# Outer-product mixer's attention on 32-key tiles: five levels and the diagonal in four column positions, the larger distances in one step

## Chip, core and metric

The kernel runs on one core of a Trainium2 chip. The metric is the device time of one execution in microseconds (us); lower is better. Before the change the median of three runs is 1098.15 us (1097.73 to 1098.18).

## What is computed

A trunk of two layers over 256 positions and 2048 channels: RMS norms, an input projection, token mixers, gates, an output projection, gated embeddings. The change touches one mixer of the first layer, `hgrn2`: eight heads with 128 key and 128 value channels. Cut to its core, for one head and a chunk of positions:

```python
f = lb + (1.0 - lb) * sigmoid(fp)          # decay per position and channel
k = (1.0 - lb) * sigmoid(-fp)
b = cumsum(log(f))
w[t, s, d] = exp(b[t, d] - b[s, d])         # s <= t, else 0
attn[t, s] = sum_d q[t, d] * k[s, d] * w[t, s, d]
o[t] = (q * exp(b))[t] @ state + attn[t] @ v
```

So the score of query t and key s carries, channel by channel, the product of the decays f at positions s+1 to t. The reference walks in chunks of 64 with a state; the kernel computes the whole lower triangle of the 256 positions instead.

## The kernel before

All large projections run on TensorE in two pieces of the operands. A weight tile `raw` arrives by DMA, ScalarE casts its high part `whi` (L123), VectorE subtracts to get the remainder `wlo` (L124). `block` (a 128-column block of output, features on partitions) runs sixteen matmuls of 512 columns with `whi` (L154), then calls `pump()`, then sixteen of 256 columns with `wlo` (L160). There are four `whi`, four `wlo` and five `raw` buffers, and a block uses two of each, so the casts run up to two blocks ahead. `merge` (L166, L167) adds the two halves. `project` is two blocks. `project_tok` (tokens on partitions, L195 to L197) pumps once for each quarter of the weights.

`pump()` is what sets the order of the work around the change. Smaller pieces of work are written as generators in lanes ("att" the attention, "rg" the linear recurrence `rg_lru`, "pl" the embeddings' norm, and others). Each pump advances every lane by one `yield`; what it issues stands on TensorE between L154 and L160 of that block. The order on each engine is then fixed by a scheduler when the program is built.

The attention runs for two groups of four heads. `attention(0)` is started before the projections of f and q for group 1 (eight blocks), and so lies between them; `attention(1)` is started after them and lies in the eight blocks of `xb_proj` and the `project_tok` of the gate (`gate_tok`), beside `rg_lru`. For one group f, q and k are 128 channels by 1024 columns, that is four heads of 256 positions, or eight chunks c of 128. The scores are built by levels: at level B the keys of the even blocks of B positions meet the queries of the odd blocks beside them, after both were scaled to the border between them by products of decays (`tot`). The steps of one group, a pump each:

- an empty one, then the diagonal: eight matmuls of 128 keys by 128 queries (L544) into two PSUM tiles `mx`, multiplied by the identity into the score tile `A` (L545), and q times f (L547);
- levels 1, 2, 4, 8 and 16: for each chunk one matmul with all 128 keys as weights and the 64 odd queries streaming (L560), then q and k are multiplied by `tot` (L567, L568), the next `tot` is made (L571), and a masked copy puts the wanted scores into `A` (L578);
- levels 32 and 64: two matmuls of 32 keys or one of 64 keys a chunk (L557), which write PSUM partitions 0 and 64, or 0; plain copies into `A` (L575);
- the cross half: keys of the first 128 positions with queries of the second (L585), copied by ScalarE to `Ac` (L587);
- `read_out`: scores times values (L608, L611), sums of squares and norm.

A float32 matmul of the program is two matmul instructions in the trace, each with a load of weights. PSUM tiles `mx` come from a pool of three, which `rg_lru` (L646, then ScalarE's sigmoids, L650) uses too.

Of the kernel before, what the change touches and what calls it, by code (L numbers as in the profile page):

```python
# [11 lines left out]
F32 = mybir.dt.float32  # L12
F32R = mybir.dt.float32r
I32 = mybir.dt.int32
U32 = mybir.dt.uint32
AF = mybir.ActivationFunctionType
ALU = mybir.AluOpType
PSUM = bass.MemoryType.PSUM

P = 128  # L20
T = 256
# [15 lines left out]
    PRM[_n] = (_o, _w)  # L37
    _o += _w
NPRM = _o
LEVELS = [1, 2, 4, 8, 16, 32, 64]  # L40
MASKED = [b for b in LEVELS if b < 32]
NCST = 128 + 64 * len(MASKED) + 256 + 64


@with_exitstack
def trunk(ctx: ExitStack, tc: tile.TileContext, a, out):
    nc = tc.nc
    v, s, gp, te, sy = nc.vector, nc.scalar, nc.gpsimd, nc.tensor, nc.sync
# [7 lines left out]
    px = ctx.enter_context(tc.tile_pool(name="px", bufs=3, space=PSUM))  # L56
# [36 lines left out]
    gp.memset(eps, EPS)  # L93
    ident = cst[:, 0:128]
    c0 = 128
    lmask = {}
    for b in MASKED:
        lmask[b] = cst[:, c0:c0 + 64].bitcast(U32)
        c0 += 64
    tri2 = cst[:, c0:c0 + 256]  # L100
    c0 += 256
    sel8 = cst[:, c0:c0 + 64].rearrange("p (h m) -> p h m", m=8)

    def pc(name, i=0, n=None):
        o, w = PRM[name]
# [289 lines left out]
    m0 = m0_scope.enter_context(tc.tile_pool(name="m0", bufs=2))  # L395
# [55 lines left out]
    def gate_tok(w, j, act, u):  # L451
# [6 lines left out]
    mx, e0, e1, lb, omb, sp, ez, z2, pol, sp8, spm8 = (small(8, n) for n in (  # L458
        "mx", "e0", "e1", "lb", "omb", "sp", "ez", "z2", "pol", "sp8", "spm8"))
# [38 lines left out]
    with m0_scope:  # L498
        ew = a["ew"]
        fs, qs, ks = [], [], []  # L500
        for g in range(2):
            f = m0.tile([P, 1024], F32, name="f", tag="f")
            k = m0.tile([P, 1024], F32, name="k", tag="k")
            q = m0.tile([P, 1024], F32, name="q", tag="q")
# [26 lines left out]

        res = {}

        def attention(g):

            f, q, k = fs[g], qs[g], ks[g]
            A = m0.tile([P, 8, P], F32, name="A", tag="A", bufs=1)
            Ac = m0.tile([P, 4, P], F32, name="Ac", tag="Ac", bufs=1)
            yield
            for b in range(2):  # L540
                ps = px.tile([P, 512], F32, name="mx", tag="mx")
                for c in range(4):
                    o = (b * 4 + c) * P
                    te.matmul(ps[:, c * P:(c + 1) * P], k[:, o:o + P], q[:, o:o + P], start=True, stop=True)  # L544
                v.tensor_tensor(out=A[:, b * 4:b * 4 + 4, :], in0=ps.rearrange("p (c t) -> p c t", c=4),  # L545
                                in1=ident.unsqueeze(1).to_broadcast([P, 4, P]), op=ALU.mult)
            v.tensor_tensor(out=q, in0=q, in1=f, op=ALU.mult)  # L547
            yield
            tot = f
            for B in LEVELS:  # L550
                ps = px.tile([P, 512], F32, name="mx", tag="mx")
                for c in range(8):
                    o = c * P
                    if B >= 32:

                        for x in range(0, P, 2 * B):
                            te.matmul(ps[x:x + B, c * 64:c * 64 + B], k[:, o + x:o + x + B],  # L557
                                      q[:, o + x + B:o + x + 2 * B], start=True, stop=True)
                    else:
                        te.matmul(ps[:, c * 64:(c + 1) * 64], k[:, o:o + P],  # L560
                                  q[:, o:o + P].rearrange("p (n two b) -> p n two b", two=2, b=B)[:, :, 1, :],
                                  start=True, stop=True)
                n = 512 // B
                tv = tot.rearrange("p (n two) -> p n two", two=2)
                qv = q.rearrange("p (n two b) -> p n two b", two=2, b=B)[:, :, 1, :]
                kv = k.rearrange("p (n two b) -> p n two b", two=2, b=B)[:, :, 0, :]
                v.tensor_tensor(out=qv, in0=qv, in1=tv[:, :, 0:1].to_broadcast([P, n, B]), op=ALU.mult)  # L567
                v.tensor_tensor(out=kv, in0=kv, in1=tv[:, :, 1:2].to_broadcast([P, n, B]), op=ALU.mult)  # L568
                if B < 64:
                    nt = m0.tile([P, n], F32, name=f"tot{B}", tag=f"tot{B}", bufs=1)  # L570
                    v.tensor_tensor(out=nt, in0=tv[:, :, 0], in1=tv[:, :, 1], op=ALU.mult)  # L571
                    tot = nt
                if B >= 32:
                    for x in range(0, P, 2 * B):
                        v.tensor_copy(A[x:x + B, :, x + B:x + 2 * B],  # L575
                                      ps.rearrange("p (c b) -> p c b", c=8)[x:x + B, :, 0:B])
                else:
                    v.copy_predicated(  # L578
                        A.rearrange("p c (n two b) -> p c n two b", two=2, b=B)[:, :, :, 1, :],
                        lmask[B].rearrange("p (n b) -> p n b", b=B).unsqueeze(1).to_broadcast([P, 8, 64 // B, B]),  # L580
                        ps.rearrange("p (c n b) -> p c n b", c=8, b=B))
                yield
            ps = px.tile([P, 512], F32, name="mx", tag="mx")
            for c in range(4):
                te.matmul(ps[:, c * P:(c + 1) * P], k[:, c * T:c * T + P], q[:, c * T + P:(c + 1) * T],  # L585
                          start=True, stop=True)
            s.copy(Ac.rearrange("p c t -> p (c t)"), ps)  # L587
            yield
            read_out(g, A, Ac, vts[g])

# [8 lines left out]

        def read_out(g, A, Ac, vt):  # L600

# [115 lines left out]
    for i in range(4):  # L717
        t = hp.tile([P, 1024], F32, name="hq", tag="h")
# [12 lines left out]
    with tc.tile_pool(name="m1", bufs=2) as m1:  # L731
# [34 lines left out]
        ps = pm.tile([P, 512], F32, name="mm", tag="mm")  # L766
        for hf in range(2):
# [124 lines left out]
        for j in range(4):  # L892
            ps = project_tok(a["oog"], j, acth)
# [132 lines left out]
        banks = []  # L1026
# [9 lines left out]
        for hf, ps in enumerate(quarter(1, [(hf, kq) for hf in range(2) for kq in range(4)])):  # L1036
            pl = pls[3][hf][:, T:2 * T]
            gated(4, ps[hf], banks[hf][:, T:2 * T], pl, hf, hf == 0)
            x = hss[:, 4, hf:hf + 1]
            p0 = pre[:, hf:hf + 1]  # L1040
            y, yh, t, r = (tp.tile([P, 1], F32, name=n, tag=n, bufs=2) for n in ("fy", "fyh", "ft", "fr"))
# [10 lines left out]
            for g in (3, 1, 0, 2):  # L1052
                o = pls[g][hf]
# [27 lines left out]
def _const():  # L1081
    c = np.zeros((P, NCST), np.float32)
    c[:, 0:128] = np.eye(P, dtype=np.float32)
    o = 128
    si = np.arange(P)[:, None]
    j = np.arange(64)[None, :]
    for b in MASKED:
        c[:, o:o + 64] = (si // (2 * b) == j // b) & ((si // b) % 2 == 0)
        o += 64
    c[:, o:o + P] = np.where(si <= np.arange(P)[None, :], 0.0, -1e30)  # L1090
    o += 256
    for h in range(8):
        c[:, o + h * 8 + h] = 1.0
    return c


# [70 lines left out]
```

## Time and profile before

| | |
|---|---|
| median of three runs | 1098.15 us |
| span of the profiled execution, first to last instruction | 1096.9 us |
| TensorE (PE) busy | 1075.8 us, 98% |
| VectorE (DVE) busy | 763.6 us, 70% |
| ScalarE (ACT) busy | 570.9 us, 52% |
| GpSimd (POOL) busy | 84.1 us, 8% |
| attention group 0 | 121 to 188 us |
| attention group 1 | 194 to 267 us |

The profiled execution's own time beside its span is not listed apart; its span is 1.25 us under the median of the runs. PE rows are matmuls, PEld rows loads of weights, which overlap with them. Matmul ends are modelled and matmuls overlap, so the distance between starts tells more than the length of one.

### The profile page before, as it was taken

The page shows a single profiled execution, that of the slowest core. Times are in us where ns is not written, and L with a number is a line of the kernel's source. Part 1 is how long each engine was busy: PE and PEld are TensorE (multiplying, and loading weights), DVE is VectorE, ACT ScalarE, POOL GpSimd, SP SyncE. Part 2 cuts the span into 40 slices and gives each one's busy share as a digit, 9 for nine tenths or more (in the row PEclk, how much of TensorE's full clock was granted, in tenths as well). Part 3 has the DMA queues.
Part 4 walks back from the last instruction along what each step waited for, and adds up shares of the span by engine and source line. Part 5 has one row for each costly group of instructions (what it writes and reads, how often), then busy time and mean ns, then how long its engine had stood idle before and what let it go on. Part 6 is the DMA issues. An engine that isn't in the chain of part 4 may idle for free.

```text
span 1096.9 us, 15476 instructions
## 1 busy us (share of the span) xinstructions
PE 1075.8 (98%) x5850; PEld 927.7 (85%) x5850; DVE 763.6 (70%) x1119; ACT 570.9 (52%) x828; POOL 84.1 (8%) x69
## 2 busy tenths in 40 slices
PE   7999999999999999999999999999999999999996
PEld 7788898988888888888888888888888877888886
DVE  7868977887877656777544877765457687655665
ACT  6565435567655435555444666554444554434443
POOL 2143200000100000112000000000000121000111
PEclk9999999999999999999999999999999999999998
DMA  8655534444765555565654654455555755555652
GB/s 322 217 180 192 183 130 151 151 135 141 240 204 186 190 192 191 189 195 172 196 196 153 197 166 154 151 167 193 192 192 191 224 201 172 192 183 182 190 175 77
DMA packets 55947, 200.37 MB, mean 183 GB/s; under 512 B 6208, under 2 KB 6464, under 8 KB 55872
## 3 DMA queue, kind: packets, MB, share of 16 engines
q1 hardware_dynamic: 54720, 195.18, 53.6%
q0 software_dynamic: 1152, 4.19, 1.2%
q8 instruction: 46, 0.75, 0.3%
q14 instruction: 29, 0.24, 0.1%
HBM read 197.25 MB, written 2.10 MB: 182 GB/s over the span
## 4 chain that ended last, share of the span: by engine, by line
PE 93%; DVE 5%; ACT 1%; issue 1%; DMA 0%; SPq 0%; DVEq 0%; ACTq 0%
PE mm L154 32%; PE mm L160 17%; PE mm L195 12%; PE mm L197 12%; PE mm L196 12%; DVE wlo L124 2%; PE mx L560 2%; PE mm L1020 1%; PE mm L1018 1%; PE mm L1019 1%; PE nu L859 1%; ACT whi L123 1%; PE mx L646 1%; DVE ahl L139 0%; DMA raw<-in_pw_dram 0%
## 5 line engine op out<-in xcount | busy, mean ns | idle before, releaser
L124 DVE TENSOR_TENSOR wlo<-raw,whi 128x1024 fp32r<-128x1024 f32 (+1 forms) x361 | 451.0, 1273 | 232.0 <-ACT whi L123 133.8
L123 ACT CAST whi<-raw 128x1024 fp32r<-128x1024 f32 (+1 forms) x361 | 376.6, 1047 | 334.9 <-PE mm L154 174.0
L154 PE MATMUL mm<-ahl,whi 128*128 128x512 f32 x1536 | 367.6, 391 | 2.7 <-DVE ahl L448 1.9
L154 PEld LDWEIGHTS mm<-ahl,whi 128*128 128x128 f32 x1536 | 282.1, 188 | 59.3 <-DVE ahl L448 3.0
L195 PE MATMUL mm<-whi,ahl 128*128 128x512 f32 x608 | 239.5, 394 | 0.8 <-DVE u L456 0.7
L197 PE MATMUL mm<-whi,ahl 128*128 128x512 f32 x608 | 236.9, 390 | 0.9 <-DVE ahl L139 0.9
L196 PE MATMUL mm<-wlo,ahl 128*128 128x512 f32 x608 | 237.1, 390 | 0.0
L160 PE MATMUL mm<-ahl,wlo 128*128 128x256 f32 x1536 | 202.3, 285 | 0.0
L160 PEld LDWEIGHTS mm<-ahl,wlo 128*128 128x128 f32 x1536 | 195.2, 191 | 6.1
L197 PEld LDWEIGHTS mm<-whi,ahl 128*128 128x128 f32 x608 | 114.1, 188 | 25.7 <-DVE ahl L139 1.8
L195 PEld LDWEIGHTS mm<-whi,ahl 128*128 128x128 f32 x608 | 114.2, 188 | 25.4 <-DVE u L456 1.5
L196 PEld LDWEIGHTS mm<-wlo,ahl 128*128 128x128 f32 x608 | 114.2, 188 | 23.4 <-DVE wlo L124 0.7
L166 ACT COPY sm<-mm 128x256 f32<-128x256 f32 x64 | 23.7, 370 | 53.7 <-PE mm L160 53.7
L272 POOL TENSOR_TENSOR acc<-acc,sq 128x512 f32<-128x512 f32 x11 | 18.1, 1642 | 214.2 <-ACT sq L271 214.0
L167 DVE TENSOR_TENSOR mg<-mm,sm 128x256 f32<-128x256 f32 x64 | 26.5, 415 | 0.1
L744 DVE SCALAR_TENSOR_TENSOR qk<-mg,prm,qk 128x255 f32<-128x255 f32 (+2 forms) x48 | 21.2, 478 | 6.9 <-ACT qk L741 6.5
L911 POOL DMA_DIRECT2D row<-in_rows_dram x4 | 2.2, 554 | 279.9 <-DVE u L943 268.1
L1006 POOL TENSOR_TENSOR pl<-pl,row 128x512 f32<-128x512 f32 x6 | 9.2, 1532 | 153.6 <-ACT sq L990 153.6
L447 ACT ACTIVATE ahl<-mx,prm 128x256 fp32r<-128x256 f32 x24 | 11.0, 473 | 18.0 <-DVE ahl L448 9.9
L560 PEld LDWEIGHTS mx<-q,k 128*128 128x128 f32 x160 | 19.4, 191 | 0.8
L560 PE MATMUL mx<-q,k 128*128 128x64 f32 x160 | 18.9, 271 | 0.0
L1018 PE MATMUL mm<-whi,ahl 128*128 128x256 f32 x64 | 18.3, 285 | 0.0
(281 smaller groups left out, 824.0 us busy)
## 6 DMA issues: line engine op xcount, KB each, us to landing
raw<-in_ew_dram SPq DMA_DIRECT2D x64, 512.0 KB, 4.5
raw<-in_g_dram SPq DMA_DIRECT2D x56, 512.0 KB, 3.9
raw<-in_eo_dram SPq DMA_DIRECT2D x32, 512.0 KB, 4.3
raw<-in_ov_dram SPq DMA_DIRECT2D x32, 512.0 KB, 3.8
raw<-in_oqk_dram SPq DMA_DIRECT2D x32, 512.0 KB, 4.2
raw<-in_oog_dram SPq DMA_DIRECT2D x32, 512.0 KB, 3.9
raw<-in_oz_dram SPq DMA_DIRECT2D x32, 512.0 KB, 3.9
raw<-in_oo_dram SPq DMA_DIRECT2D x32, 512.0 KB, 4.3
```

The lines of the kernel that those rows point to most:

```text
L123: last["act"] = s.copy(h, r).ins
L124: last["dve"] = v.tensor_tensor(out=l, in0=r, in1=h.bitcast(F32), op=ALU.subtract).ins
L154: last["pe"] = te.matmul(ps, parts[k // 8][0][:, c:c + P], act[k // 2][2][:, (k % 2) * 512:(k % 2 + 1) * 512], start=(k == 0), stop=False).ins
L160: last["pe"] = te.matmul(ps[:, T:2 * T], parts[k // 8][1][:, c:c + P], act[k // 2][0][:, k % 2], start=False, stop=(k == KT - 1)).ins
L166: s.copy(small, ps[:, T:2 * T])
L167: v.tensor_tensor(out=dst, in0=ps[:, 0:T], in1=small, op=ALU.add)
L195: te.matmul(ps[hf], xh, wh, start=(k == 0), stop=False)
L196: te.matmul(ps[hf], xh, wl, start=False, stop=False)
L197: last["pe"] = te.matmul(ps[hf], xl, wh, start=False, stop=(k == KT - 1)).ins
L560: te.matmul(ps[:, c * 64:(c + 1) * 64], k[:, o:o + P], q[:, o:o + P].rearrange("p (n two b) -> p n two b", two=2, b=B)[:, :, 1, :], start= ...
L744: v.scalar_tensor_tensor(dst[:, sh:T], pi[:, 0:T - sh], pc("ccw", k * 16 + b), dst[:, sh:T], op0=ALU.mult, op1=ALU.add)
L1018: te.matmul(ps[hf], xh, wh, start=(k == 0), stop=False)
```

## The change

The last two levels go, and the diagonal moves into the first level. Everything within 32 positions is now computed on tiles of 32 keys: a matmul has 32 keys as weights, streams 16 queries (32 for the diagonal), and writes one of four groups of 32 PSUM partitions (the column positions 0, 32, 64 and 96 of the array). Their results go to a small tile `C` of 32 columns a chunk, by masked copies of 128 columns in all, and ScalarE copies `C` into the diagonal blocks of `A`. The last step does all larger distances at once: pairs of neighbouring 32-blocks straight from k and qf, blocks two and three apart with copies scaled once more (`k64`, `q64`, which reuse the tile of `tot`), and the cross half with copies `kx`, `qx` (which reuse f), scaled by running products of the four decays of a half (`sx`, `pf`, first filled by GpSimd). q times f goes to a tile of its own, `qf`. `A` is made once, zeroed by GpSimd. A group now takes eight pumps instead of eleven.

```diff
-LEVELS = [1, 2, 4, 8, 16, 32, 64]
+LEVELS = [1, 2, 4, 8, 16]
...
+        A = m0.tile([P, 8, P], F32, name="A", tag="A", bufs=1)
+        gp.memset(A, 0.0)
...
-            for b in range(2):
-                ps = px.tile([P, 512], F32, name="mx", tag="mx")
-                for c in range(4):
-                    te.matmul(ps[:, c * P:(c + 1) * P], k[:, o:o + P], q[:, o:o + P], start=True, stop=True)
-                v.tensor_tensor(out=A[:, b * 4:b * 4 + 4, :], in0=ps.rearrange("p (c t) -> p c t", c=4),
-                                in1=ident.unsqueeze(1).to_broadcast([P, 4, P]), op=ALU.mult)
-            v.tensor_tensor(out=q, in0=q, in1=f, op=ALU.mult)
+            v.tensor_tensor(out=qf, in0=q, in1=f, op=ALU.mult)
             yield
...
+                if B == 1:
+                    for c in range(8):
+                        for x in range(0, P, 32):
+                            o = c * P + x
+                            te.matmul(ps[x:x + 32, 128 + c * 32:160 + c * 32], k[:, o:o + 32], q[:, o:o + 32],
+                                      start=True, stop=True)
                 for c in range(8):
-                    if B >= 32:
-                        for x in range(0, P, 2 * B):
-                            te.matmul(ps[x:x + B, c * 64:c * 64 + B], k[:, o + x:o + x + B],
-                                      q[:, o + x + B:o + x + 2 * B], start=True, stop=True)
-                    else:
-                        te.matmul(ps[:, c * 64:(c + 1) * 64], k[:, o:o + P],
-                                  q[:, o:o + P].rearrange("p (n two b) -> p n two b", two=2, b=B)[:, :, 1, :],
+                    for x in range(0, P, 32):
+                        o = c * P + x
+                        te.matmul(ps[x:x + 32, c * 16:(c + 1) * 16], k[:, o:o + 32],
+                                  qf[:, o:o + 32].rearrange("p (n two b) -> p n two b", two=2, b=B)[:, :, 1, :],
                                   start=True, stop=True)
...
+            for x in range(0, P, 32):
+                s.copy(A[x:x + 32, :, x:x + 32], C[x:x + 32])
+            yield
+            for b in range(2):
+                ps = px.tile([P, 512], F32, name="mx", tag="mx")
+                for i in range(4):
+                    c = 4 * b + i
+                    for x, kk, y_, qq in ((0, k4[:, c, 0], 1, q4[:, c, 1]), (1, k4[:, c, 1], 2, q4[:, c, 2]),
+                                          (2, k4[:, c, 2], 3, q4[:, c, 3]), (0, k64[:, c], 2, q4[:, c, 2]),
+                                          (1, k4[:, c, 1], 3, q64[:, c]), (0, k64[:, c], 3, q64[:, c])):
+                        te.matmul(p3[32 * x:32 * x + 32, i, 32 * y_:32 * y_ + 32], kk, qq, start=True, stop=True)
...
+                te.matmul(ps[:, cc], kx[:, cc], qx[:, cc], start=True, stop=True)
+            for b, p3 in enumerate(banks):
+                for x in range(3):
+                    r = slice(32 * x, 32 * x + 32)
+                    s.copy(A[r, 4 * b:4 * b + 4, 32 * x + 32:P], p3[r, :, 32 * x + 32:P])
             s.copy(Ac.rearrange("p c t -> p (c t)"), ps)
             yield
             read_out(g, A, Ac, vts[g])
```

TensorE at the end of group 0, from level 16 on, before (a row is line, operation, output and inputs, shape of the output, count of matmuls of the program; `mm` rows are the projection's):

```order
L560 MATMUL mx<-q,k 128x64 x8
L160 MATMUL mm<-ahl,wlo 128x256 x16
L154 MATMUL mm<-ahl,whi 128x512 x16
L557 MATMUL mx<-q,k 32x32 x16
L160 MATMUL mm<-ahl,wlo 128x256 x16
L154 MATMUL mm<-ahl,whi 128x512 x16
L557 MATMUL mx<-q,k 64x64 x8
L160 MATMUL mm<-ahl,wlo 128x256 x16
L154 MATMUL mm<-ahl,whi 128x512 x16
L585 MATMUL mx<-q,k 128x128 x4
```

The same place now, with the first of the last step's eight chunks (`tot_1344` is the tile of `k64` and `q64`; line numbers are those of the changed kernel, where the projection's L154 and L160 are L153 and L159):

```order
L556 MATMUL mx<-qf,k 32x16 x32
L159 MATMUL mm<-ahl,wlo 128x256 x16
L153 MATMUL mm<-ahl,whi 128x512 x16
L615 MATMUL mx<-qf,k 32x32 x3
L615 MATMUL mx<-qf,tot_1344 32x32
L615 MATMUL mx<-tot_1344,k 32x32
L615 MATMUL mx<-tot_1344 32x32
```

Two pumps with a block each have gone from between level 16 and the cross half. The blocks themselves are as many as before, so they now stand elsewhere: what follows in the lane comes earlier.

ScalarE in group 1 around the cross half, before (`it` and `av` are `rg_lru`'s sigmoids, `u` the gate's, `tt` its tanh, `whi` the casts of weights):

```order
L650 ACTIVATE it<-mx,prm 128x256 x2
L123 CAST whi<-raw 128x1024
L455 ACTIVATE u<-mm,rth 128x512
L587 COPY Ac<-mx 128x512
L656 ACTIVATE tt<-av,sp_257 128x256 x2
L657 ACT_TABLE_LOAD
L657 ACTIVATE av<-av,spm_258 128x256
L123 CAST whi<-raw 128x1024 x2
```

And now, from the second bank's copies to the next cast of weights:

```order
L624 COPY A<-mx 32x4x96
L624 COPY A<-mx 32x4x64
L624 COPY A<-mx 32x4x32
L625 COPY Ac<-mx 128x512
L694 ACTIVATE tt<-av,sp_257 128x256
L688 ACT_TABLE_LOAD
L688 ACTIVATE av<-mx,prm 128x256 x2
L688 ACTIVATE it<-mx,prm 128x256 x2
L165 COPY sm<-mm 128x256
L695 ACT_TABLE_LOAD
L695 ACTIVATE av<-av,spm_258 128x256
L122 CAST whi<-raw 128x1024
```

The cross half of group 1 moved from the gate's first tiles back between the blocks of `xb_proj`, into the middle of `rg_lru`'s activations, and three copies for each bank stand ahead of `Ac`.

More of the change, by code (lines that the diff above doesn't have):

```diff
@@ L95, in trunk @@
     c0 = 128
+    ident32 = cst[:, c0:c0 + 32]
+    c0 += 32
     lmask = {}
-    for b in MASKED:
-        lmask[b] = cst[:, c0:c0 + 64].bitcast(U32)
-        c0 += 64
+    for b in LEVELS:
+        lmask[b] = cst[:, c0:c0 + 16].bitcast(U32)
+        c0 += 16
     tri2 = cst[:, c0:c0 + 256]
-    c0 += 256
-    sel8 = cst[:, c0:c0 + 64].rearrange("p (h m) -> p h m", m=8)
     def pc(name, i=0, n=None):
@@ L568, in attention @@
                 v.tensor_tensor(out=kv, in0=kv, in1=tv[:, :, 1:2].to_broadcast([P, n, B]), op=ALU.mult)
[L569 to L581, printed above, removed]
@@ L582, in attention @@
-                yield
+                nt = m0.tile([P, n], F32, name=f"tot{B}", tag=f"tot{B}", bufs=1)
+                v.tensor_tensor(out=nt, in0=tv[:, :, 0], in1=tv[:, :, 1], op=ALU.mult)
+                if B == 1:
+                    v.tensor_tensor(out=C, in0=ps[:, 128:384].rearrange("p (c t) -> p c t", c=8),
+                                    in1=ident32.unsqueeze(1).to_broadcast([P, 8, 32]), op=ALU.mult)
+                    t1 = nt
+                tot = nt
+                v.copy_predicated(
+                    C.rearrange("p c (n two b) -> p c n two b", two=2, b=B)[:, :, :, 1, :],
+                    lmask[B].rearrange("p (n b) -> p n b", b=B).unsqueeze(1).to_broadcast([P, 8, 16 // B, B]),
+                    ps[:, 0:128].rearrange("p (c n b) -> p c n b", c=8, b=B))
@@ new lines, in attention @@
+                if B < 16:
+                    yield
+            tb = tot.rearrange("p (c b) -> p c b", b=4)
+            t4 = tot.rearrange("p (h two b) -> p h two b", two=2, b=4)
+            sx = m0.tile([P, 4, 4], F32, name="sx", tag="sx", bufs=1)
+            pf = m0.tile([P, 4, 4], F32, name="pf", tag="pf", bufs=1)
+            gp.memset(sx[:, :, 3:4], 1.0)
+            gp.memset(pf[:, :, 0:1], 1.0)
+            v.tensor_copy(sx[:, :, 2], t4[:, :, 0, 3])
+            v.tensor_copy(pf[:, :, 1], t4[:, :, 1, 0])
@@ new lines, in attention @@
+            for i in (1, 0):
+                v.tensor_tensor(out=sx[:, :, i], in0=sx[:, :, i + 1], in1=t4[:, :, 0, i + 1], op=ALU.mult)
+                j = 3 - i
+                v.tensor_tensor(out=pf[:, :, j], in0=pf[:, :, j - 1], in1=t4[:, :, 1, j - 1], op=ALU.mult)
+            k64, q64 = (t1[:, i * T:(i + 1) * T].rearrange("p (c s) -> p c s", s=32) for i in range(2))
+            kx, qx = (f[:, i * 512:(i + 1) * 512] for i in range(2))
+            k4 = k.rearrange("p (c b s) -> p c b s", b=4, s=32)
@@ new lines, in attention @@
+            q4 = qf.rearrange("p (c b s) -> p c b s", b=4, s=32)
+            k5 = k.rearrange("p (h two b s) -> p h two b s", two=2, b=4, s=32)
+            q5 = qf.rearrange("p (h two b s) -> p h two b s", two=2, b=4, s=32)
+            v.tensor_tensor(out=k64, in0=k4[:, :, 0], in1=tb[:, :, 1:2].to_broadcast([P, 8, 32]), op=ALU.mult)
+            v.tensor_tensor(out=q64, in0=q4[:, :, 3], in1=tb[:, :, 2:3].to_broadcast([P, 8, 32]), op=ALU.mult)
+            v.tensor_tensor(out=kx.rearrange("p (h b s) -> p h b s", h=4, s=32), in0=k5[:, :, 0],
+                            in1=sx.unsqueeze(3).to_broadcast([P, 4, 4, 32]), op=ALU.mult)
@@ L1085, in _const @@
     si = np.arange(P)[:, None]
[L1086 to L1089, printed above, removed]
+    j = np.arange(16)[None, :]
+    c[:, o:o + 32] = si % 32 == np.arange(32)[None, :]
+    o += 32
+    for b in LEVELS:
+        c[:, o:o + 16] = (si % 32 // (2 * b) == j // b) & ((si // b) % 2 == 0)
+        o += 16
     c[:, o:o + P] = np.where(si <= np.arange(P)[None, :], 0.0, -1e30)
-    o += 256
-    for h in range(8):
-        c[:, o + h * 8 + h] = 1.0
     return c
```

20 lines of the change are left out of this document (11 added, 9 removed).

## Prediction

> **What bounds the kernel now.** I read the page first: its totals, the share of each engine, and the chain that ended last.
>
> ```profile
> span 1096.9 us, 15476 instructions
> PE 1075.8 (98%) x5850; PEld 927.7 (85%) x5850; DVE 763.6 (70%) x1119; ACT 570.9 (52%) x828; POOL 84.1 (8%) x69
> PE 93%; DVE 5%; ACT 1%; issue 1%; DMA 0%; SPq 0%; DVEq 0%; ACTq 0%
> ```
>
> TensorE is busy in 98% of the span and carries 93% of the chain, so work taken off it shortens the kernel wherever nothing else is late. Next I read the chain in order of time through the attention, where each step stands between the sixteen L154 and the sixteen L160 matmuls of a projection block (columns: start, length, what).
>
> ```profile
> 112.58 3.65 PE mm L154 x16
> 116.23 1.91 PE mm L160 x16
> 118.14 3.66 PE mm L154 x16
> 121.80 1.78 PE mx L544 x16
> ...
> 125.49 3.65 PE mm L154 x16
> 129.15 1.73 PE mx L560 x16
> ...
> 132.84 3.65 PE mm L154 x16
> ...
> 162.22 3.65 PE mm L154 x16
> 165.88 0.63 PE mx L557 x32
> 166.51 2.11 PE mm L160 x16
> 168.62 3.65 PE mm L154 x16
> 172.27 1.08 PE mx L557 x16
> ...
> 175.46 3.65 PE mm L154 x16
> 179.11 0.89 PE mx L585 x8
> ...
> 181.91 3.65 PE mm L154 x16
> ...
> 248.01 2.20 DVE tt L668
> ```
>
> Every link from 112 to 182 us is TensorE: the vector work of a step lies wholly beside the blocks. From one L154 to the next a block without a step takes 118.14 - 112.58 = 5.56. With the diagonal step it takes 7.35 (125.49 - 118.14), with a level of full 128-column weights also 7.35 (132.84 - 125.49), with B = 32 it takes 6.40, with B = 64 6.84, with the cross half 6.45 (181.91 - 175.46). So the steps cost 1.79, 1.79, 0.84, 1.28 and 0.89. A group pays the diagonal, five levels and the last three: 6 x 1.79 + 0.84 + 1.28 + 0.89 = 13.75 us. In group 1 the chain leaves TensorE for a while: the last row is VectorE's scan of rg_lru, and what the attention wants next stands behind it.
>
> **TensorE, the main term.** A float32 matmul of the program is two matmul instructions in the trace (16 matmuls of B = 32 are x32). After the change a group issues 32 + 32 matmuls in its first step (128 instructions), 32 in each of four levels (64 each), and 48 (96 instructions) and the cross half in the last. What one instruction with 32 columns of weights costs is read from B = 32, its neighbour with 64 columns beside it. First the timeline of PE (start, length from first to last end), then the groups by shape (count | busy, mean ns of one | idle before).
>
> ```profile
> 165.81 0.70 PE L557 MATMUL mx<-q,k 128*32 128x32 f32 x32
> 172.20 1.15 PE L557 MATMUL mx<-q,k 128*64 128x64 f32 x16
> ```
>
> ```profile
> L560 PE MATMUL mx<-q,k 128*128 128x64 f32 x112 | 13.2, 271 | 0.0
> L557 PE MATMUL mx<-q,k 128*64 128x64 f32 x32 | 2.3, 224 | 1.0 <-DVE tot L571 1.0
> L557 PE MATMUL mx<-q,k 128*32 128x32 f32 x64 | 1.4, 197 | 0.0
> ```
>
> Thirty-two starts and one length of 0.197 fill 0.70, so the starts are (0.70 - 0.197) / 31 = 16.2 ns apart. With 64 columns of weights they are (1.15 - 0.224) / 15 = 61.7 ns apart, and with 128 columns 13.2 / 112 = 118, although both of these stream the same 64 columns. So the columns of weights set the pace, about 31 ns for 32 of them at one position; B = 32 alternates between two positions (partitions 0 and 64) and gets half of that. I take the same 16.2 ns for the new tiles: streaming 16 columns instead of 32 gains nothing where weights set the pace. Nor do four positions gain on two, because the two instructions of one matmul stand next to each other at the same position, so only neighbours in the stream can overlap. What a step pays beside its starts is 0.84 - 32 x 0.0162 = 0.32, of which 0.20 shows in the following L160 row, 2.11 instead of 1.91.
>
> - A level: 64 x 0.0162 + 0.32 = 1.36 for 1.79; four of them save 1.72.
> - First step (diagonal and B = 1 together): 128 x 0.0162 + 0.32 = 2.39 for 2 x 1.79 = 3.58; saves 1.19.
> - Last step: 96 x 0.0162 + 0.32 + 0.89 for the cross half = 2.77. Each of the eight chunks ends and begins at position 0, where neighbours can't overlap: 8 x 0.016 = 0.13, so 2.90 for 0.84 + 1.28 + 0.89 = 3.01; saves 0.11.
>
> That is 3.02 a group, 6.0 us for both. The bounds on the pace are 8 ns (four positions at once, 31 / 4) and 31 ns (no overlap); 16.2 is the row of the same weights, so I take it.
>
> The Trainium skill speaks against this edit: TensorE: Matmul & The Clock Gate, Back-to-back issue gap, gives matmuls of 1 to 64 columns a floor of about 25 ns from start to start. By 25 ns a group would cost 4 x 1.92 + 3.52 + 3.61 = 14.81, and the kernel would lose 2.1 us on TensorE instead of gaining 6.0. The L557 row, at 16.2 ns over 32 starts, lies under that floor.
>
> **VectorE and ScalarE.** Their rows by shape, then the stretches of the two groups (busy us and counts).
>
> ```profile
> L578 DVE COPY_PREDICATED A<-cst,mx 128x512 f32<-128x512 uint32 x10 | 9.6, 957 | 0.0
> L567 DVE TENSOR_TENSOR q<-q,tot 128x512 f32<-128x512 f32 x12 | 8.3, 689 | 11.4 <-PE mx L560 9.2 <-PE mx L557 2.2
> L571 DVE TENSOR_TENSOR tot<-tot 128x256 f32<-128x256 f32 x2 | 0.8, 410 | 0.0
> L209 DVE SCALAR_TENSOR_TENSOR hnr<-hnt,hnr 128x8 f32<-128x8 f32 x3 | 0.5, 167 | 0.1
> L124 DVE TENSOR_TENSOR wlo<-raw,whi 128x1024 fp32r<-128x1024 f32 x45 | 56.2, 1284 | 9.4 <-ACT whi L123 4.2 <-ACT Ac L587 3.0 <-PE mm L160 1.9
> L166 ACT COPY sm<-mm 128x256 f32<-128x256 f32 x17 | 6.3, 371 | 23.8 <-PE mm L160 23.8
> L615 ACT ACTIVATE sq<-mx 128x128 f32<-128x128 f32 x12 | 3.2, 277 | 0.0
> L615 ACT ACTIVATION_READ_ACCUMULATOR sq<-mx 128x1 f32 x12 | 2.5, 207 | 0.0
> L612 ACT COPY o<-mx 128x512 f32<-128x512 f32 x3 | 1.7, 578 | 0.0
> 110.00:193.00 83.00, 83.00 (x561) 74.57 (x561) 66.59 (x98) 37.53 (x64) 5.40 (x3) 1.00 0.47 157
> 193.00:266.00 73.00, 72.02 (x458) 63.40 (x457) 59.95 (x94) 46.62 (x73) 1.90 (x1) 1.00 0.41 135
> ```
>
> VectorE loses, per group, two diagonal products (2 x 0.69, priced by L567), two levels of multiplications (4 x 0.69), 5 x (0.96 - 0.41) of masked copies that shrink from 512 columns to 128 (priced at 256, so with care), and three plain copies (2 x 0.41 and one of 512 columns, 0.69): 8.4 us. It gains the small diagonal and two scalings of 256 columns (3 x 0.41), two of 512 (2 x 0.69) and eight tiny operations (8 x 0.17): 4.0. Four us less per group are worth nothing beside TensorE, except where B = 64 waits in group 1, 1.0 us by its row above. That step is gone, and group 1 reads out five pumps earlier, ahead of the late scan. I count 1.0 gained; the bounds are 0 and 1.0.
>
> What is late next? In the B = 16 step VectorE must finish q and k (2 x 0.69), two weight remainders (2 x 1.28), the last masked copy (0.41 at most) and the two scalings for distance 64 (2 x 0.41) before the last step: 5.2 us, against 1.91 + 3.65 = 5.56 of block. The two 512-column products are wanted only by the cross half, 1.6 us further on, and take 1.4. It fits with about 0.4 us to spare; if not, the matmuls wait that much, and the L160 block behind them.
>
> ScalarE takes over the copies: four of 256 columns (4 x 0.37) and six of 384, 256 and 128 (2 x (0.47 + 0.37 + 0.28), between L166 and L612) make 3.7 us a group. In group 0 it is idle for 45 of 83 us. In group 1 the last step takes three PSUM buffers of mx, and rg_lru, next on TensorE, wants one when its first three copies have run: 1.1 us of copies, beside 0.8 for the second bank's matmuls and 0.9 for the cross half. That covers them if ScalarE is free at once; it comes from casts and activations, so I charge 0.3 us; bounds 0 and 1.1. POOL's two fills of sx and pf (its span is almost empty) and the smaller constant load stand early and cost nothing; if POOL's fills came late, the tiny products would wait, but only behind ple_norm's products, which end before group 1's step.
>
> Sum: -6.0 - 1.0 + 0.3 = -6.7 us on a span of 1096.9, which gives 1090.2. The median of the three runs, 1098.15, lies 1.25 above that span; with it the forecast is **1091.4 us**. About 0.2% (2.2 us) is what a measurement of this kernel can tell from no change.
>
> **The rivals.**
>
> - *Long runs fall behind (chance 0.14).* 16.2 ns is seen only over 32 starts; runs are now 64 to 128 long. If each instruction costs what B = 32 cost all in, 0.84 / 32 = 26 ns with no fixed part, a level is 1.68, the first step 3.36, the last 3.41: 13.49 for 13.75. Saved 0.5 in all, with the other terms 1.2: 1096.9 (0.10). With the 0.32 of a step kept beside such a pace a group costs 4 x 1.98 + 3.65 + 3.71 = 15.28, 3.1 more for both: 1100.5 (0.04). For it: nothing in the trace runs so densely for so long. Against: 31 starts in 0.50 us already went faster. By the 25 ns of the Trainium skill's TensorE: Matmul & The Clock Gate it would be 2.1 - 0.7 = 1.4 slower, 1099.6.
> - *Neighbouring positions don't overlap: slower (0.07).* Positions 0 and 64 did, 32 apart hasn't been seen. At 31 ns a group costs 488 x 0.031 + 6 x 0.32 + 0.89 = 17.9, 4.2 more; both 8.4, less 0.7: 1105.8. It turns from gain to loss at a pace of 23 ns ((13.75 + 0.35 - 2.81) / 488).
> - *ScalarE becomes late in group 1 (0.18).* The last step now falls between rg_lru's activations, and the read-out follows at once: 2 x 0.58 + 8 x (0.28 + 0.21) = 5.0 us that before ran beside the gate. With the 3.7 of copies that is 8.7 us ahead of casts that feed the gate's first tiles; ScalarE was busy for 46.6 of 73 us there, so two blocks (11.1 us) leave about 4 free and cast two tiles ahead cover the rest. If they don't, 2 to 4 us come back: 1093.4 to 1095.4.
> - *Four positions run at once (0.06).* 8 ns: a group costs 488 x 0.008 + 2.81 = 6.7, 7.0 less; 1083.4. The Trainium skill's TensorEngine Tiling (Array Packing), Theoretical Speedup, allows up to four times for a dimension of 32. Against it stands the pair of instructions at one position.
>
> **How the numbers follow.** The forecast case has 0.55 (1088.5 to 1093.4 with its bounds: 2 ns of pace either way are 2 us). Range 1088.5 to 1097.0: the forecast, ScalarE's case and the better half of the long runs, 0.8 together. Faster by over 0.2%: 0.55 + 0.18 + 0.06, less a little for what isn't seen here, 0.77; within: 0.13, mostly the long runs; slower: 0.10.
>
> **What would show it.** In the profile after: 64-instruction levels that take about 1.2 us from first start to last end, a first step of 2.3, a chain that stays on TensorE through group 0, no wait of the 32-row matmuls for VectorE. A pace over 23 ns in those groups, or the first gate tiles waiting for whi or wlo, makes the forecast wrong. A start of the attention moved by more than 1 us would be the reordered loads, which I count at zero.

## The result and the profile after

The changed kernel takes 1091.03 us (median of four runs, 1089.92 to 1091.62) where the kernel before takes 1097.94 (1096.97 to 1098.18): ratio 0.9932, 95% interval 0.9920 to 0.9944. The profiled execution took 1090.81 us with a span of 1089.0. The forecast was 1091.4. That it came out so near is luck: two terms were wrong in opposite directions, and the trace shows both.

First the page of the changed kernel: its totals and the chain that ended last.

```profile
span 1089.0 us, 16844 instructions
PE 1064.6 (98%) x6522; PEld 913.0 (84%) x6522; DVE 753.4 (69%) x1121; ACT 580.8 (53%) x850; POOL 86.5 (8%) x74
PE 89%; DVE 5%; ACT 4%; issue 1%; DMA 1%; SPq 0%; DVEq 0%; ACTq 0%
```

TensorE is still busy for 98% of the span, but its share of the chain fell from 93% to 89% and ScalarE's rose from 1% to 4%. So ScalarE now holds a part of this chain that it didn't hold before. Next, the chain in order of time through group 0 (start, length, what). L153 and L159 are the two halves of a projection block, L154 and L160 before.

```profile
118.90 3.65 PE mm L153 x16
122.55 0.66 PE mx L551 x49
...
123.24 0.52 PE mx L556 x32
123.76 2.11 PE mm L159 x16
125.87 3.65 PE mm L153 x16
129.52 0.67 PE mx L556 x51
130.19 2.11 PE mm L159 x16
132.30 3.65 PE mm L153 x16
...
151.56 3.65 PE mm L153 x16
155.22 1.63 PE mx L615 x89
156.85 1.09 PE mx L620 x8
...
159.86 0.23 PE mm L153
```

A block without a step takes 5.56. So the first step costs 125.87 - 118.90 - 5.56 = 1.41 us, a level 132.30 - 125.87 - 5.56 = 0.87, the last step 159.86 - 151.56 - 5.56 = 2.74. A group comes to 4 x 0.87 + 1.41 + 2.74 = 7.63 us for 13.75: 6.1 saved, 12.2 in both groups. The forecast had 6.0 in both. The timeline says why (start, length from first start to last end):

```profile
129.45 0.74 PE L556 MATMUL mx<-qf,k 128*32 128x16 f32 x64
```

One instruction lasts 0.185 us, so 64 of them are (0.74 - 0.185) / 63 = 8.8 ns apart, not the 16.2 that I took. The B = 64 wait of 1.0 us is gone with its step. That would have made the span 13.2 us shorter, but it is 7.9 shorter. The rest was given back in two places. The waits of TensorE between 200 and 275 us, in group 1's last steps and rg_lru, are (total, times, longest):

```profile
PE mm L194 <- DVE u L455: 1.2, 1, 1.2
PE mm L195 <- DVE wlo L123: 0.8, 1, 0.8
PE mx L684 <- ACT A L624: 0.5, 1, 0.5
PE mm L194 <- ACT whi L122: 0.5, 1, 0.5
```

Counted from start to start (the distance between the two matmuls around a wait, less the usual one), these are 1.41, 1.03, 0.68 and 0.65 us, and two of group 1's levels start 0.15 and 0.17 us late, behind VectorE: 4.1 in all. And the attention begins later. Two rows of the timeline frame the stretch in which the two kernels differ: the first matmul of the attention, and the second set of transposes of gated values (L438, L439 before).

```profile
121.64 1.95 PE L544 MATMUL mx<-q,k 128*128 128x128 f32 x16
301.49 1.04 PE L439 MATMUL mx<-cst,u 128*128 128x128 f32 x8
```

```profile
122.48 0.73 PE L551 MATMUL mx<-q,k 128*32 128x32 f32 x62
293.65 1.03 PE L438 MATMUL mx<-cst,u 128*128 128x128 f32 x8
```

The stretch shrank from 179.85 to 171.17 us, by 8.68; the start in front of it moved by +0.84; and behind it both kernels take the same (1096.9 - 301.49 = 795.4, and 1089.0 - 293.65 = 795.4). I use this stretch below, because it leaves out what the start does from execution to execution.

### The profile page after: what moved, and what is told of

Its sections match the earlier page's. It is cut to its first block, busy times and chain, and to the rows that moved or that the text cites. A ratio compares the mean times of both kernels' runs of the same rounds, so it can differ in the third digit from the quotient of the medians.

```text
span 1089.0 us, 16844 instructions
## 1 busy us (share of the span) xinstructions
PE 1064.6 (98%) x6522; PEld 913.0 (84%) x6522; DVE 753.4 (69%) x1121; ACT 580.8 (53%) x850; POOL 86.5 (8%) x74
## 4 chain that ended last, share of the span: by engine, by line
PE 89%; DVE 5%; ACT 4%; issue 1%; DMA 1%; SPq 0%; DVEq 0%; ACTq 0%
PE mm L153 31%; PE mm L159 17%; PE mm L194 12%; PE mm L196 12%; PE mm L195 12%; DVE wlo L123 2%; ACT whi L122 1%; PE mm L1058 1%; PE mm L1056 1%; PE mm L1057 1%; DMA raw<-in_pw_dram 1%; PE nu L897 1%; PE mx L556 1%; DVE ahl L138 0%; ACT L695 0%
## 5 line engine op out<-in xcount | busy, mean ns | idle before, releaser
L153 PE MATMUL mm<-ahl,whi 128*128 128x512 f32 x1536 | 367.7, 392 | 2.7 <-DVE ahl L447 1.9
L153 PEld LDWEIGHTS mm<-ahl,whi 128*128 128x128 f32 x1536 | 282.3, 188 | 59.1 <-DVE ahl L447 3.0
L194 PE MATMUL mm<-whi,ahl 128*128 128x512 f32 x608 | 239.8, 394 | 2.4 <-DVE u L455 1.9
L159 PE MATMUL mm<-ahl,wlo 128*128 128x256 f32 x1536 | 202.4, 285 | 0.0
L159 PEld LDWEIGHTS mm<-ahl,wlo 128*128 128x128 f32 x1536 | 195.4, 191 | 6.2
L194 PEld LDWEIGHTS mm<-whi,ahl 128*128 128x128 f32 x608 | 114.3, 188 | 27.6 <-DVE u L455 3.1
L138 DVE TENSOR_TENSOR ahl<-hq,ahl 128x512 fp32r<-128x512 f32 x16 | 10.7, 690 | 10.8 <-ACT ahl L137 10.8
L1057 PE MATMUL mm<-wlo,ahl 128*128 128x256 f32 x64 | 18.1, 283 | 0.0
```

The lines of the kernel that those rows point to most:

```text
L153: last["pe"] = te.matmul(ps, parts[k // 8][0][:, c:c + P], act[k // 2][2][:, (k % 2) * 512:(k % 2 + 1) * 512], start=(k == 0), stop=False).ins
L159: last["pe"] = te.matmul(ps[:, T:2 * T], parts[k // 8][1][:, c:c + P], act[k // 2][0][:, k % 2], start=False, stop=(k == KT - 1)).ins
L194: te.matmul(ps[hf], xh, wh, start=(k == 0), stop=False)
L1057: te.matmul(ps[hf], xh, wl, start=False, stop=False)
```

## The experiments

Each kernel is the changed one with one edit, except the tiles alone (an edit of the kernel before) and the combinations at the end. Each was timed against the kernel before. The stretch is worked out as above from the timeline of each kernel's profiled execution. The 95% intervals are some 3 us wide, so differences of 1 to 2 us between these kernels are read from the stretch; the kernel with 656 columns, which differs from the changed one only in the size of a load at the start and the order of the early work, has the same stretch to 0.01 us.

| kernel | us, median (runs from, to) | ratio to before, 95% interval | start of attention | stretch |
|---|---|---|---|---|
| changed | 1091.03 (1089.92, 1091.62) | 0.9932 [0.9920, 0.9944] | 122.48 | 171.17 |
| one position at a time | 1104.63 (1104.15, 1105.5) | 1.0059 [1.0044, 1.0074] | 122.97 | 184.66 |
| two positions | 1095.51 (1094.53, 1095.78) | 0.9975 [0.9964, 0.9986] | 123.32 | 175.07 |
| each position twice | 1091.23 (1091.12, 1092.43) | 0.9936 [0.9919, 0.9952] | 123.38 | 171.97 |
| tiles alone | 1090.93 (1089.74, 1092.2) | 0.9933 [0.9919, 0.9948] | 121.57 | 171.94 |
| late read-out | 1089.01 (1088.29, 1089.17) | 0.9911 [0.9896, 0.9925] | 123.04 | 168.73 |
| late last step | 1090.51 (1090.1, 1090.63) | 0.9924 [0.9908, 0.9941] | 123.09 | 170.40 |
| copies on VectorE | 1089.91 (1089.66, 1091.15) | 0.9922 [0.9908, 0.9937] | 123.60 | 170.41 |
| 656 columns of constants | 1092.03 (1091.14, 1092.8) | 0.9939 [0.9924, 0.9954] | 123.69 | 171.17 |
| second buffer for it | 1088.22 (1087.32, 1089.43) | 0.9908 [0.9893, 0.9923] | 123.36 | 167.87 |
| 768 columns of constants | 1089.59 (1089.0, 1090.96) | 0.9922 [0.9907, 0.9936] | 121.48 | 170.30 |
| three together | 1087.11 (1085.05, 1087.43) | 0.9893 [0.9876, 0.9909] | 122.57 | 167.13 |
| three, and late read-out | 1085.40 (1085.27, 1085.71) | 0.9886 [0.9869, 0.9902] | 120.77 | 167.41 |

### What sets the pace of the tiles

My theory from the trace of the changed kernel: matmuls at distinct column positions that stand next to each other in the stream run as a batch. Three kernels change only the order in which the same matmuls of the levels (and, in the same way, of the diagonal) are issued.

**One position at a time.**

```diff
-                for c in range(8):
-                    for x in range(0, P, 32):
+                for x in range(0, P, 32):
+                    for c in range(8):
                         o = c * P + x
```

> The five levels and the diagonal issue all matmuls of one column position before those of the next, so a neighbour in the stream has nearly always the same position. Batch theory (matmuls at distinct positions, next to each other in the stream, run together, first their first instructions, then their second; a batch takes 2 x 31.6 ns whatever the number of positions in it): 31.6 ns an instruction, a level's 64 starts take 2.0 us instead of 0.5, a group costs 9.1 us more on TensorE, the kernel 14 to 18 us more than the changed one: 1105 to 1109 us. Theory that the position doesn't matter, and that 32 columns of weights and a short stream simply go at 7.9 ns: no change, 1091.

**Two positions.**

```diff
-                for c in range(8):
-                    for x in range(0, P, 32):
+                for c, x in [(c, x + y) for x in (0, 32) for c in range(8) for y in (0, 64)]:
+                    if True:
```

> The matmuls of levels and diagonal alternate between partitions 0 and 64, then between 32 and 96. Batch theory: two to a batch, 15.8 ns an instruction, a level's run 1.0 us instead of 0.5, 3.0 us more on TensorE in each group: 1094 to 1097 us. The prediction's theory (the two instructions of one matmul have the same position, so only one neighbour overlaps, and two positions do as well as four): the same pace as the changed kernel, 1091.

**Each position twice in a row.**

```diff
-                for c in range(8):
-                    for x in range(0, P, 32):
+                for c, x in [(c + d, x) for c in range(0, 8, 2) for x in range(0, P, 32) for d in (0, 1)]:
+                    if True:
```

> Each position is used by two matmuls in a row before the next (0, 0, 32, 32, 64, 64, 96, 96). Batch theory, strictly in order: a repeated position ends the batch, so four batches carry eight matmuls: 15.8 ns an instruction, a level's run 1.0 us, 1094 to 1097 us. Rival (each position has a queue of its own that holds some matmuls, so that order within a few doesn't matter): 7.9 ns, 1091.

One level of group 0 from the timeline of each of the three kernels, in this order:

```profile
132.19 1.90 PE L556 MATMUL mx<-qf,k 128*32 128x16 f32 x64
```

```profile
130.94 1.10 PE L556 MATMUL mx<-qf,k 128*32 128x16 f32 x64
```

```profile
130.53 0.83 PE L556 MATMUL mx<-qf,k 128*32 128x16 f32 x64
```

The starts are 27.2, 14.5 and 10.2 ns apart, beside 8.8 in the changed kernel. So the position does matter, and the pace goes with the number of positions in use: the theory that 32 columns of weights and a short stream simply go fast is out. Four positions gain over two, against the prediction's step. The batch theory foresaw 31.6 ns and 1105 to 1109 us for the first run, a little more than came (1104.63). The third run is a plain miss for it. In strict order each repeated position would end a batch, and the pace would be 15.8; it is 10.2, and the time that of the rival. What fits is that each position takes its matmuls one after another, while matmuls at other positions that stand near in the stream go on; then the busiest position sets the pace. In the one-position run most starts are 31 to 32 ns apart (less where the position changes), so a matmul of two instructions takes about 63 ns of its position. In the changed kernel a level has 8 matmuls at each position: 8 x 63 = 0.50 us, and its starts spread over 0.55. The last step has 24 of its 48 at position 0: 24 x 63 = 1.51, and its 96 starts are 15.9 ns apart, 1.51 us. With each position twice in a row the starts of a level spread over 0.65, also for 8 matmuls at each, so the order still costs something. How far ahead a matmul at a free position may go is not settled by these runs.

The one-position run also says something on group 1. Its levels are 13.5 us longer over the stretch, yet its four waits there are those of the changed kernel, the two longest among them:

```profile
PE mm L194 <- DVE u L455: 1.2, 1, 1.2
PE mm L195 <- DVE wlo L123: 0.8, 1, 0.8
```

More time beside the levels doesn't shrink them, so they aren't a lack of such time.

### The tiles alone

The kernel before, with only the matmuls of the five levels on 32-key tiles. The masked copy reads the four tiles of a bank in four pieces.

```diff
-                        te.matmul(ps[:, c * 64:(c + 1) * 64], k[:, o:o + P],
-                                  q[:, o:o + P].rearrange("p (n two b) -> p n two b", two=2, b=B)[:, :, 1, :],
-                                  start=True, stop=True)
+                        for x in range(0, P, 32):
+                            te.matmul(ps[x:x + 32, c * 64 + x // 2:c * 64 + x // 2 + 16], k[:, o + x:o + x + 32],
+                                      q[:, o + x:o + x + 32].rearrange("p (n two b) -> p n two b", two=2, b=B)[:, :, 1, :],
+                                      start=True, stop=True)
...
-                    v.copy_predicated(
+                    for x in range(0, P, 32):
+                        r, h = slice(x, x + 32), slice(x // 2, x // 2 + 16)
+                        v.copy_predicated(
...
```

> The kernel before, in which only the matmuls of the five levels 1 to 16 become 32-key tiles at four positions (the masked copy of a level reads the four tiles as four copies of 32 partitions); diagonal, 32, 64, cross half, read-out and ScalarE's work stay. Theory that TensorE's pace is the gain and ScalarE's new work in group 1 takes part of it back: ten levels of 0.87 instead of 1.79 give 9.2 us, and with nothing new on ScalarE nearly all of it shows: 1088 to 1090 us, less than the whole change. Rival (the whole change's loss in group 1 comes from less time beside TensorE there, whoever does the copies): 1091 to 1093.

It took 1090.93 us, between the two expectations and equal to the whole change. Its stretch is 7.91 us shorter than before, of the 9.2 that ten levels save. TensorE's waits in group 1 are two, both for VectorE, where the kernel before had one of 1.0; that is about 0.4 of the difference, and the rest isn't placed:

```profile
PE mx L557 <- DVE tot L572: 0.8, 1, 0.8
PE mx L649 <- DVE A L581: 0.6, 1, 0.6
```

So the small diagonal, the merged last step and the copies on ScalarE, which save TensorE another 3.0 us and the B = 64 wait, earned only 0.8 us in the stretch (171.17 for 171.94), and nothing in the time, as the attention of the changed kernel started 0.91 later. The next runs ask where that went.

### Group 1: too much work, or one wait?

In the changed kernel ScalarE's timeline of that time has these rows (start, length; in brackets the idle time and what ended it):

```profile
239.01 1.05 ACT L122 CAST whi<-raw 128x1024 fp32r<-128x1024 f32 x1 [1.40 <-PE mm L196]
243.40 0.47 ACT L688 ACTIVATE it<-mx,prm 128x256 f32<-128x256 f32 x1 [3.33 <-DVE tt L706]
243.77 1.04 ACT L122 CAST whi<-raw 128x1024 fp32r<-128x1024 f32 x1
...
252.59 1.28 ACT L695 ACT_TABLE_LOAD   x1
...
255.10 1.03 ACT L122 CAST whi<-raw 128x1024 fp32r<-128x1024 f32 x1
```

ScalarE stands 3.33 us at the first write of rg_lru's second `it`. That tile has one buffer, and VectorE's scan of the first call (L706) hasn't read it yet. Behind this write, in ScalarE's own order, are sigmoids, exponentials with their table loads, and the casts that the gate's matmuls want at 255 to 260. Two explanations: ScalarE has too much to do (the prediction's rival: read-out, copies, activations), or it has enough time and loses it at this one write. Four kernels tell them apart.

**Late read-out, and late last step.** The read-out of group 1 comes four pumps later; in the second kernel the last step does.

```diff
             s.copy(Ac.rearrange("p c t -> p (c t)"), ps)
-            yield
+            for _ in range(5 if g else 1):
+                yield
             read_out(g, A, Ac, vts[g])
```

```diff
                 s.copy(A[x:x + 32, :, x:x + 32], C[x:x + 32])
-            yield
+            for _ in range(5 if g else 1):
+                yield
             banks = []
```

> The changed kernel with the read-out of group 1 four pumps later, among the gate's matmuls. Theory (ScalarE is late in group 1 because the copies, the read-out and rg_lru's activations come together; about 4.3 us of TensorE are lost there): the read-out is 5.0 us of ScalarE, and without it 2 to 4 us come back: 1087 to 1089 us. Rival (the table loads and VectorE's chain through rg_lru's scan are the cause): 1090.5 to 1091.5, with the same waits at L194 and L195.

> As the run before, but the last step of group 1 (pairs and cross half, with its seven copies) is late by four pumps too. Theory: rg_lru finds its PSUM buffers free (0.68 us at L684 gone) and ScalarE has 3 us less to do ahead of the gate: 1087 to 1088.5 us. Rival: the late step meets rg_lru's second half and the gate's activations, and the waits only move: 1090 to 1092.

**Copies on VectorE.**

```diff
-                s.copy(A[x:x + 32, :, x:x + 32], C[x:x + 32])
+                (v.tensor_copy if g else s.copy)(A[x:x + 32, :, x:x + 32], C[x:x + 32])
...
-                    s.copy(A[r, 4 * b:4 * b + 4, 32 * x + 32:P], p3[r, :, 32 * x + 32:P])
+                    (v.tensor_copy if g else s.copy)(A[r, 4 * b:4 * b + 4, 32 * x + 32:P], p3[r, :, 32 * x + 32:P])
```

> Group 1's ten copies into A on VectorE instead of ScalarE; nothing moves in time. Theory (ScalarE's lateness): 3.6 us less on ScalarE, 1 to 3 us come back, 1088 to 1090 us. Rival (VectorE is as late there, waits for wlo and for u show it): no gain or a loss, 1091 to 1093.

**Second buffer for it.** No work is removed. The second call writes `it` where the attention's `qf` was.

```diff
-            it = m0.tile([P, 1024], F32, name="it", tag="it", bufs=1)
+            it = m0.tile([P, 1024], F32, name="it", tag="qf" if r else "it", bufs=1)
```

> The changed kernel in which rg_lru's second call writes its gate it into the buffer that the attention's qf leaves free, instead of the one buffer that the first call's scan still reads. In the changed kernel ScalarE stands 3.3 us at this write (it waits for VectorE's scan), with the casts behind it. Theory (this wait, with three table loads behind it, is what makes the gate's casts late): the waits of 1.03 and 1.41 us at L195 and L194 shrink or go, 1 to 2.5 us come back: 1088.5 to 1090 us. Rival (ScalarE simply has too much to do, and waits elsewhere instead): 1090.5 to 1091.5.

TensorE's waits between 200 and 275 us with the copies on VectorE, then with the second buffer (its only one):

```profile
PE mm L194 <- DVE u L455: 1.3, 1, 1.3
PE mm L195 <- DVE wlo L123: 0.8, 1, 0.8
PE mm L194 <- ACT whi L122: 0.2, 1, 0.2
```

```profile
PE mx L684 <- ACT A L624: 0.5, 1, 0.5
```

Taking the ten copies off ScalarE removed the wait of rg_lru for PSUM buffers (L684) and left the gate's waits nearly as they were. Its 1.1 us of time lie in the expected interval, but not for the expected reason. The second buffer took nothing off ScalarE, not one table load (nine between 193 and 266 us in both kernels), and all three gate waits went: the stretch is 3.30 us shorter, against 1.41 + 1.03 + 0.65 = 3.1 counted, and the time, 1088.22, lies a little under the theory's interval. Two of its rows on ScalarE, the write of `it` (now without a stop) and the cast that stood at 255.10:

```profile
238.49 0.48 ACT L688 ACTIVATE it<-mx,prm 128x256 f32<-128x256 f32 x1
252.72 1.03 ACT L122 CAST whi<-raw 128x1024 fp32r<-128x1024 f32 x1
```

The edit also made the scheduler swap a few neighbours in ScalarE's order; this cast stands behind one more activation (L695) than before. Even so it comes 3.26 us earlier, counted from the start of the attention in each kernel, which is the length of the stop. So it is the one wait, not the work. The late read-out came to 1089.01 us, the edge of its theory's interval, but it too works by the wait: it gains 2.44 in the stretch because the scan then starts at 235.9 instead of 241.1 and the write that waits for it is nearly on time; at L194 0.6 of wait is left. The late last step is its rival's case: the waits only move, to the step itself (0.8, for a sigmoid ahead of it), to rg_lru's next matmuls and to the gate.

The kernel before had the same stop, and TensorE lost only the 1.0 of B = 64 in that time:

```profile
ACT it L650 <- DVE tt L668: 3.5, 1, 3.5
```

With the tiles alone ScalarE stood there 0.3.

### The start

The attention began 0.84 us later in the changed kernel. Two kernels pad the constant load.

```diff
-NCST = 128 + 32 + 16 * len(LEVELS) + 256
+NCST = 656
```

> The changed kernel with the constant load padded from 496 to 656 columns (of 768 before). The attention's first block started 0.76 us later in the changed kernel. If the smaller load (it ends earlier and lets the weight loads behind it start at another time) is the cause, the start moves back by some 0.4 us; if it is chance between executions or the reordered early work, the start stays within 0.2 us of the changed kernel's, or moves by as much in the other runs as well. Time 1090.5 to 1091.5 in either case.

```diff
-NCST = 128 + 32 + 16 * len(LEVELS) + 256
+NCST = 768
...
-            Ac = m0.tile([P, 4, P], F32, name="Ac", tag="Ac", bufs=1)
+            Ac = q[:, 0:512].rearrange("p (c t) -> p c t", c=4)
```

> The changed kernel with the constant load padded to the 768 columns that it had before (Ac stands in q's buffer, to make room). With 768 columns the first ninety operations of VectorE stand in the order of the kernel before, and so do ScalarE's but for one cast; with 656 (the run before) they did not. Theory (the order of the early casts and splits, which the length of this load sets, moves the start): the attention's first matmul, 122.5 us in the changed kernel and 123.0 to 123.7 in its other variants, comes at 121.5 to 122.0, and the time falls by 0.8 to 1.5 us: 1089.5 to 1090.3. Rival (chance): start over 122.4, time 1090.8 to 1091.5.

The 656 columns were a miss: the start was the latest of all (123.69) and the time above both expectations. With 768 the start came at 121.48 and the time 1.4 us lower, both in the theory's intervals. But only part of it is the start: the stretch is 0.87 shorter too, with ScalarE's stop at `it` 2.5 us instead of 3.3, and why this edit shortens it is open. TensorE's longest wait between 20 and 50 us in the changed kernel, with 656 and with 768 columns:

```profile
PE mm L196 <- DVE ahl L138: 1.8, 2, 1.1
```

```profile
PE mm L194 <- ACT ahl L137: 1.6, 2, 1.3
```

```profile
PE mm L196 <- DVE ahl L138: 0.2, 1, 0.2
```

In the first projection the order in which ScalarE and VectorE split activations (ahl) and weights decides how long TensorE waits for ahl, and that order changes with the length of the load (it differs between 496, 656 and 768 columns), and a longer load isn't always better. With the order of before it is 0.2 or less in four kernels of five (0.9 in the kernel before). The changed kernel and the kernel before were level at the 21st matmul instruction (11.03 and 11.07 us), so it is these waits, 1.8 for 0.9, that make up the 0.84. So about 1 us of the later start comes with the change, through the order that the scheduler chose. Other differences of the start don't come from that order: with the order of before, the start came at 120.77, 121.48 and 122.57 in three kernels, and the 21st matmul instruction already at 10.83, 11.70 and 12.74.

### All of it together

The three edits (768 columns, second buffer, copies on VectorE), and then the late read-out with them.

> The two runs before in one, with group 1's copies into A on VectorE as well. If the three causes (early order, wait for the scan, copies that hold PSUM buffers) add up: 1.2 + 1.1 + 1 to 2.5 us off 1091.0, so 1086.2 to 1087.7 us. If two of them are covers of the same time in group 1: 1088 to 1089.5.

> The three edits of the run before with the late read-out of group 1 as well. Theory (the late read-out alone gained 2.0 us only because ScalarE and VectorE reach rg_lru's scan some 5 us earlier, so that the wait of the second gate for it ends earlier; the second buffer takes that wait away, so both gain the same time): within 0.6 us of the three together, 1086.5 to 1087.7 us; TensorE's waits left in group 1 there are 0.2 to 0.3 us each, about 1 us in all. Rival (the 5 us of read-out on ScalarE cost time of their own): 1 to 2 us more off, 1085.0 to 1086.2 us.

The three together took 1087.11 us, and no wait of TensorE between 200 and 275 us is left in the view. The stretch is 4.04 shorter than in the changed kernel. Alone, the second buffer gained 3.30 and the copies 0.76, 4.06 in sum, so these two add up; the 0.87 that the 768 columns gained in the stretch don't come on top. The two late levels (0.15 and 0.17) are still there. With the late read-out the time was 1085.40, inside the rival's interval. The rows of the timeline say otherwise, first of the three together, then with the late read-out:

```profile
122.57 0.73 PE L551 MATMUL mx<-q,k 128*32 128x32 f32 x62
289.70 1.03 PE L438 MATMUL mx<-cst,u 128*128 128x128 f32 x8
```

```profile
120.77 0.73 PE L551 MATMUL mx<-q,k 128*32 128x32 f32 x62
288.18 1.04 PE L438 MATMUL mx<-cst,u 128*128 128x128 f32 x8
```

The stretch is 167.13 and 167.41: the read-out's place gains nothing once the second buffer is there, as the theory said. The difference lies in the first 20 us, ahead of anything that these edits touch. Either version beats the changed kernel and the kernel before; between the two I don't choose.

## Why the prediction was right, and by which errors

| term, us on the span | forecast | measured |
|---|---|---|
| TensorE, both groups | -6.0 | -12.2 |
| B = 64 wait of group 1 | -1.0 | -1.0 |
| rg_lru's wait for PSUM buffers | +0.3 | +0.7 |
| ScalarE and VectorE late in group 1 | 0 (a rival, +2 to 4) | +3.1, and 0.3 at two levels |
| start of the attention | 0 | +0.8 |
| sum | -6.7 | -8.3 |
| span | -6.7 | -7.9 |

The measured terms leave 0.4 us that I can't place. By its own signs the forecast was wrong although its number came out: a level took 0.74 us from first start to last end and not 1.2, and the gate's first tiles waited for whi and wlo.

**The pace, wrong.** The step that failed: "Nor do four positions gain on two, because the two instructions of one matmul stand next to each other at the same position, so only neighbours in the stream can overlap." The runs put in its place that each position takes about 63 ns a matmul, and that positions work at once: 27.2, 14.5 and 8.8 ns between starts for one, two and four. So TensorE saved 12.2 us where the sum had 6.0. The row of B = 32 couldn't tell this from a rule of neighbours, since it alternates between just two positions; both rules give 16 ns there. I took that row as the price and gave the case of four at once 0.06. The fixed part of a step held: 0.87 - 64 x 0.0088 = 0.31, for the 0.32 taken. That 16 streamed columns gain nothing on 32 held too: the 128 starts of the first step, half of them with 32 columns, are 8.7 ns apart. (The 118 ns read for 128 columns of weights is busy time per instruction; the starts of those rows are 108 apart, and the sum doesn't use it.) The last step was near (2.74 for 2.90), as position 0's share of the work keeps it at 15.9 ns.

The Trainium skill's TensorE: Matmul & The Clock Gate, Back-to-back issue gap, gives matmuls of 1 to 64 streamed columns a floor of about 25 ns; the mean pace at one position keeps to it (27.2), and two and four positions go under it (14.5 and 8.8). The Trainium skill's TensorEngine Tiling (Array Packing), Theoretical Speedup, allows up to four times for a dimension of 32; here the pace rose 27.2 / 8.8 = 3.1 times.

**ScalarE late in group 1, half right.** The rival's size (2 to 4 us) and place (the gate's first tiles, waiting for whi and wlo) are what happened, on top of a larger gain. Its cause isn't: I counted 8.7 us of ScalarE's work against its free time, while the loss is one write that waits for a buffer that VectorE still reads. The trace of before showed that row too, 3.5 us long, and I didn't ask who would stand behind it when the steps move up.

**Smaller steps.** The copies were priced at 3.7 us a group and took 4 x 0.40 + 2 x (0.46 + 0.36 + 0.26) = 3.8. They covered the PSUM wait less well than thought, 0.7 for 0.3, inside its bounds. VectorE's B = 16 step fitted in both groups; instead the matmuls of B = 4 and of B = 16 in group 1 came 0.15 and 0.17 late behind VectorE. The smaller load was counted at nothing and cost about 1 us through the order of the early work. Long runs didn't fall behind, and neighbouring positions overlap.

## What to carry to other kernels

A measured pace holds for the pattern that it was measured in: ask which of the possible rules gave it, and what each would give for the new pattern. Before adding up an engine's work, look in the trace for the instruction on it that stands and waits, and list what is queued behind it; a second buffer there was worth 3.3 us, taking 3.8 us of work off the engine 0.8. And compare kernels over a stretch between two rows that both have, since the start of the execution alone differed by up to 2 us between kernels with the same early order.

## What was not expected of the hardware

- Matmuls with 32 columns of weights at four column positions start 8.8 ns apart, at two 14.5, at one 27.2; using each position twice in a row costs little (10.2).
- With 16 or 32 streamed columns the starts of such matmuls are equally dense (8.7 ns over the 128 starts of the first step, half of them with 32 columns, and 8.8 in a level).
- The 21st matmul instruction of the program came between 10.83 and 12.74 us in kernels with the same early order of work, while what follows the stretch took 795.4 us in the kernel before and in the changed one alike.
